# A two-block network on one core: value products of head pairs in turns, the residual written out, the RWKV mixer in 64x64 quarters

## The chip, the core and the metric

The kernel runs on one core of a Trainium2 chip. The core has five engines with a queue each: TensorE (PE, the matrix array; PEld in the profile is its weight load), VectorE (DVE), ScalarE (ACT), GpSimd (POOL) and SyncE (SP), which here issues the DMA transfers between memory (HBM) and the on-chip memory SBUF. Results of PE go to the eight banks of PSUM. The metric is the device time of one execution in microseconds, as the median of several.

## The reference, cut to what matters

A sequence of 512 tokens of width 1024 goes through two blocks of two layers. A layer of the first block joins neighbourhood attention (NA), grouped-query attention and a spatial gating; one of the second block joins four mixers, RWKV-7 among them, and a dense or an expert feed-forward part. What the change touches:

```python
def neighbourhood_attention(q, k, v, rpb):      # 8 heads of 64
    ...
    scores = scores + bias.astype(jnp.float32)
    scores = jnp.where(col_valid[:, None, :], scores, jnp.float32(-1e30))
    ...
    out = jnp.einsum('bhrqjk,brjkhd->brqhd', p, vg)
...
def gqa_attention(q, k, v):                     # 8 query heads, 2 key/value heads of 64
    ...
        sc = jnp.einsum('bqkgd,bskd->bkgqs', qi, k).astype(jnp.float32) * scale
        p = jax.nn.softmax(sc, axis=-1).astype(v.dtype)
        return jnp.einsum('bkgqs,bskd->bqkgd', p, v)
...
    return layer_norm(DEEPNORM_ALPHA * x + sub, ln_g, ln_b)   # x: the residual
...
def _rwkv7_scan(r, w, k, v, kk, a):             # 4 heads of 64, token by token
    ...
        sa = jnp.einsum('bhvk,bhk->bhv', state, -kkt)
        state = (state * wt[:, :, None, :]
                 + sa[..., None] * (kkt * at)[:, :, None, :]
                 + vt[..., None] * kt[:, :, None, :])
        return state, jnp.einsum('bhvk,bhk->bhv', state, rt)
```

## The kernel before, in words

Activations are held transposed (channels on the 128 partitions, 512 tokens along a row). All projections run as three products of split halves (`mm3`, lines 398 to 400: high by high, low by high, high by low), written `mm<-hh,wh`, `mm<-hl,wh`, `mm<-hh,wl` in the trace, with weights that SP loads in pieces of 128x1024 (`wr`) and ACT and DVE split (lines 387, 391). The core products of the mixers and attentions are fp32; such a matmul stands in the trace as two rows, a projection's as one.

Python generators issue the work: `weave` runs several side by side, each with a weight, and advances the one whose yielded costs are furthest behind its weight. A scheduler then sets the order within each engine's queue from what is ready, save where `issue_after` forces it. SP issues all loads in the order in which the program gives them; a load whose buffer is still in use holds up those behind it.

Attention. In each layer of the first block the NA stage (98 to 252 us, layer one) is woven with the projections for the other branches, the grouped-query stage (252 to 502 us) with two output branches and the spatial gating. Heads go in pairs, tokens in four blocks `a` of 128. `av_pair` scales the probabilities of both heads, transposes them (tp, line 837), copies them to `tmp` and multiplies them with the values (line 846, written `av<-tmp,gvt` or `av<-tmp,navt`): head u writes the column half u of the array, 4 key blocks in the grouped-query stage, 2 or 3 in NA. NA also needs a bias for each head, two loads `nab` that POOL negates (lines 622, 623), issued at the start of the pair that uses them. The residual H, eight tiles of 128x512, stays in SBUF over the whole layer; only the last norm of the first block writes it to memory (`spill`), after POOL has added the output bias (line 510).

RWKV. In each layer of the second block the mixer's two head pairs R(0) and R(1) are woven with the projections of two other mixers (1318 to 1500 us in layer one, 2182 to 2360 in layer two). It works on eight chunks of 64 tokens. For each head a score matrix SB over blocks of 128 tokens is made (line 1610 masks it), then the inverse of a unit triangular matrix by five doubling steps: Yp = SB T (`sc<-T,SB`), copied by DVE and ACT to Y (line 1637), Z = Y Tt (`av<-T,Y`), merged into Tt by a predicated copy of DVE (line 1642), and Tt transposed to T again (line 1647, `tp<-cst,T`). T and Tt share a tile, so the trace names both T. The tiles at, bt, rt and kt are shown as cum, a and e. Behind the loop come the products for W, G and ND, seven state steps ST (`sc<-ST,G`), further scores, and the output products `op` (`av<-SB,W`, `av<-SB,vT`, `av<-e,ST`). All these go through `mm`, line 1495.

Of the kernel before, what the change touches and what calls it, by code (L numbers as in the profile page):

```python
# [19 lines left out]
P = 128  # L20
# [19 lines left out]
RW = 58  # L40
# [9 lines left out]
SY, IY, YE, TE = 0.92, (0.5, 0.35, 0.5), (0, 1), (0, 1)  # L50
# [90 lines left out]
def host_arrays(inp):  # L141
# [25 lines left out]
    a["cst2"], a["msk2"] = _consts2()  # L167
    a["pos"] = np.ascontiguousarray(inp["positions_2"].reshape(1, S))
# [67 lines left out]
def _consts2():  # L236
# [19 lines left out]
    return np.ascontiguousarray(f), np.ascontiguousarray(np.concatenate(m, 1).astype(np.float32))  # L256

# [49 lines left out]
class K:  # L307
# [214 lines left out]

    def stats(self):
        return self.xp.tile([P, 4, 4, 6], F32, name="st", tag="st", bufs=2)


    def first_block(self):
# [9 lines left out]
        self.ln.bo = self.row(R_L + 2)  # L537
# [22 lines left out]
    def hybrid(self, l, hT):  # L560
# [51 lines left out]
        def na_attention():  # L612
            ahead = Ahead()
            nxt = both(nq[0]), *twice(nk[0])
            for i in range(4):
                av = self.bank("av")
                qs, kh, kl = nxt
                bts, mx, sm = [], [], []
                for u in range(2):
                    b0 = self.load(aps[f"nab_{l}"][2 * i + u][:, 0:384], "nab")  # L620
                    b1 = self.load(aps[f"nab_{l}"][2 * i + u][:, 384:896], "nab")
                    nc.gpsimd.tensor_scalar(b0[:, :384], b0[:, :384], -1.0, None, op0=ALU.mult)
                    nc.gpsimd.tensor_scalar(b1, b1, -1.0, None, op0=ALU.mult)
                    bts.append((b1[:, 0:256], b0[:, 0:384], b0[:, 0:384], b1[:, 256:512]))
                    x, y = stats()
                    mx.append(x)
                    sm.append(y)
                for a in range(4):
# [18 lines left out]
                    yield NY  # L647

# [163 lines left out]
        self.norm_begin(nb, nb + 1, nb + 5 + 2 if l + 1 < DEPTH else None, spill=l + 1 == DEPTH)  # L812
# [13 lines left out]
    def av_pair(self, av, a, pts, sms, nb, v):  # L826
# [5 lines left out]
        for u, (pt, sm) in enumerate(zip(pts, sms)):  # L832
# [9 lines left out]
            else:  # L842
                nc.vector.tensor_copy(t[:, :n], tp[:, :n])
        for b in range(nb):
            for u in range(2):
                nc.tensor.matmul(av[64 * u:64 * u + 64, a * P:(a + 1) * P], v(u, b), pT[u][:, b * P:(b + 1) * P],
                                 start=b == 0, stop=b == nb - 1)


    def second_block(self, hT):  # L850
# [12 lines left out]
        m64 = self.cp.tile([P, 7, 64], mybir.dt.uint8, name="m64")  # L863
        self.ident64 = self.cp.tile([P, 64], F32, name="ident64")
        for h in (slice(0, 64), slice(64, P)):
            nc.gpsimd.tensor_copy(m64[h], msk[h, :7 * P].rearrange("p (n c) -> p n c", c=P)[:, :, h])
            nc.gpsimd.tensor_copy(self.ident64[h], self.ident[h, h])
        self.lv64 = m64[:, 0]
        self.lvt64 = lambda n: m64[:, 1 + n]
# [463 lines left out]
    def mixers(self, l, hT):  # L1333
# [73 lines left out]
        def out_projection():  # L1407
            self.H = [[self.load(self.hd[j][t * P:(t + 1) * P, :], "H") for j in range(2)] for t in range(4)]
# [116 lines left out]
    def rwkv_pair(self, i, r, k, v, wa, g1, s2z):  # L1525
# [71 lines left out]

        two = [slice(0, 64), slice(64, P)]
        v64 = lambda x: x[:, :4 * 64].rearrange("p (t c) -> p t c", c=64)
        bc64 = lambda m: m.unsqueeze(1).to_broadcast([m.shape[0], 4, 64])  # L1600
        copy = (nc.scalar.copy, nc.vector.tensor_copy, nc.gpsimd.tensor_copy)
        SB, T, Tt, Y = {}, {}, {}, {}

        def score(u, w):
            x, y = ((bt, at), (bt, rt), (kt, at), (kt, rt))[w]
            ps = self.bank("sc")
            for t in range(4):
                self.mm(q(ps, t), q(x, t)[two[u]], q(y, t)[two[u]])
            z_ = self.c("SB")
            nc.vector.tensor_mul(v4(z_), v4(ps), bc4(self.masks[w % 2]))  # L1610
            return z_

        for u in range(2):
            rr = two[u]
            z_ = self.c("T")
            T[u], Tt[u] = z_[:, :256], z_[:, 256:]
            nc.gpsimd.tensor_copy(v64(T[u]), bc64(self.ident64))
            nc.gpsimd.tensor_copy(v64(Tt[u]), bc64(self.ident64))
            Y[u] = self.c("Y")
            nc.gpsimd.memset(Y[u], 0.0)  # L1620
            SB[u] = [score(u, 0)]
            yield SY
            lp = self.bank("tp")
            for t in range(4):
                nc.tensor.transpose(q(lp, t), q(SB[u][0], t), self.ident)
            for h in two:
                nc.vector.copy_predicated(v64(Tt[u])[h], bc64(self.lvt64(0)[h]), v4(SB[u][0])[h, :, h])
                nc.vector.copy_predicated(v64(T[u])[h], bc64(self.lv64[h]), v4(lp)[h, :, h])
            yield 0.5
        for n in range(1, 6):  # L1630
            for u in range(2):
# [331 lines left out]
```

## Time and profile before

| | us |
|---|---|
| median of three runs | 3246.71 (3242.65 to 3255.93) |
| profiled execution, its own time | 3253.21 |
| span of the profiled execution | 3251.4 |
| PE busy in it | 3102.4 (95%) |
| DVE busy | 1909.2 (59%) |
| ACT busy | 1338.0 (41%) |
| POOL busy | 364.0 (11%) |

The mean granted clock of PE is 0.975 of full speed. The profile lists for each engine how long it was busy; its timeline gives each instruction's start and duration, runs of equal ones on one row with their count, and in brackets how long the engine stood idle ahead of it and what released it. Durations of matmuls overlap with the next one, so the time that one takes up is read from starts.

### The profile page before, as it was taken

To read this page: it belongs to the slowest core of one execution; us is meant where nothing else is said; L and a number is where in the kernel's file an instruction comes from. 1 tells how busy PE (TensorE), PEld (TensorE's weight loads), DVE (VectorE), ACT (ScalarE), POOL (GpSimd) and SP (SyncE) were. 2 spreads that over 40 slices of the span, in tenths; PEclk is the share of its full clock that TensorE was granted. 3 is DMA by queue.
4 is the path that set the end of the run, shared out by engine and by line. 5 is a ranking of instruction groups with operands and counts; after the bars stand their busy time and mean duration, and the time that the engine had idled before them with its cause. 6 is when DMAs were issued, how large, how long until landed. Compare 5 with 4: busy or idle time off the path is not lost. (4 is left out here: it accounts for less than half of the span.)

```text
span 3251.4 us, 44427 instructions
## 1 busy us (share of the span) xinstructions
PE 3102.4 (95%) x17353; PEld 2503.6 (77%) x17353; DVE 1909.2 (59%) x3414; ACT 1338.0 (41%) x2315; POOL 364.0 (11%) x400
## 2 busy tenths in 40 slices
PE   7999999999999999999999999999999899999997
PEld 5687778877777787886657888779775588989983
DVE  6666544657745566735564333556266667777775
ACT  3534333335333333524433222343253366666652
POOL 3120000201100001003300000200042110000021
PEclk9999999999999999999999999999999899999997
DMA  4222123232221333100202333321012167877782
GB/s 160 86 84 78 59 65 115 77 114 74 83 78 58 102 105 113 57 27 27 98 20 91 92 98 99 130 80 40 27 31 90 62 225 259 257 250 257 247 285 92
DMA packets 111627, 356.87 MB, mean 110 GB/s; under 512 B 12913, under 2 KB 15985, under 8 KB 111409
## 3 DMA queue, kind: packets, MB, share of 16 engines
q1 hardware_dynamic: 108528, 344.51, 32.5%
q0 software_dynamic: 2880, 9.44, 0.8%
q8 instruction: 138, 2.26, 0.3%
q14 instruction: 81, 0.66, 0.1%
HBM read 340.40 MB, written 13.50 MB: 109 GB/s over the span
## 5 line engine op out<-in xcount | busy, mean ns | idle before, releaser
L391 DVE TENSOR_TENSOR wl<-wr,wh 128x1024 fp32r<-128x1024 f32 (+1 forms) x574 | 698.5, 1225 | 513.9 <-ACT wh L387 498.3
L387 ACT CAST wh<-wr 128x1024 fp32r<-128x1024 f32 (+1 forms) x574 | 594.2, 1045 | 754.4 <-PE mm L399 369.4
L398 PE MATMUL mm<-hh,wh 128*128 128x512 f32 (+1 forms) x1616 | 652.7, 404 | 1.3 <-DVE tmp L1462 1.2
L399 PE MATMUL mm<-hl,wh 128*128 128x512 f32 (+1 forms) x1616 | 643.9, 398 | 0.0
L400 PE MATMUL mm<-hh,wl 128*128 128x512 f32 (+1 forms) x1616 | 642.3, 398 | 0.0
L398 PEld LDWEIGHTS mm<-hh,wh 128*128 128x128 f32 (+1 forms) x1616 | 305.4, 189 | 75.8 <-issue 11.7
L400 PEld LDWEIGHTS mm<-hh,wl 128*128 128x128 f32 (+1 forms) x1616 | 305.2, 189 | 71.7 <-issue 4.2
L399 PEld LDWEIGHTS mm<-hl,wh 128*128 128x128 f32 (+1 forms) x1616 | 305.6, 189 | 70.2 <-issue 6.9
L1240 PE MATMUL mm<-xgT,wh 128*128 128x320 f32 x704 | 218.4, 310 | 0.5 <-ACT wh L387 0.3
L1240 PE MATMUL sc<-xgT,wh 128*128 128x320 f32 x704 | 218.1, 310 | 0.1
L1241 PE MATMUL mm<-xgT,wl 128*128 128x256 f32 x704 | 198.3, 282 | 4.0 <-DVE wl L391 4.0
L1241 PE MATMUL sc<-xgT,wl 128*128 128x256 f32 x704 | 196.9, 280 | 0.0
L1241 PEld LDWEIGHTS mm<-xgT,wl 128*128 128x128 f32 x704 | 132.6, 188 | 6.3 <-DVE wl L391 5.9
L431 POOL TENSOR_TENSOR rs<-rs,mhalf 128x1 f32<-128x1 f32 x36 | 32.0, 890 | 917.0 <-DVE rs L430 880.8
L1240 PEld LDWEIGHTS mm<-xgT,wh 128*128 128x128 f32 x704 | 132.7, 189 | 1.8 <-DVE xgT L1219 0.6
L1240 PEld LDWEIGHTS sc<-xgT,wh 128*128 128x128 f32 x704 | 132.5, 188 | 0.3 <-DVE tmp L1246 0.3
L1241 PEld LDWEIGHTS sc<-xgT,wl 128*128 128x128 f32 x704 | 132.7, 188 | 0.0
L398 PE MATMUL mm<-wh,hh 128*128 128x256 f32 x448 | 131.9, 294 | 0.0
L399 PE MATMUL mm<-wl,hh 128*128 128x256 f32 x448 | 130.3, 291 | 0.3 <-DVE wl L391 0.3
L400 PE MATMUL mm<-wh,hl 128*128 128x256 f32 x448 | 128.3, 286 | 0.0
L709 DVE TENSOR_REDUCE mn<-sc 128x1 f32<-128x512 f32 x64 | 44.0, 688 | 89.6 <-PE sc L706 89.6
L399 PEld LDWEIGHTS mm<-wl,hh 128*128 128x128 f32 x448 | 86.1, 192 | 5.8 <-issue 4.4
(553 smaller groups left out, 5929.1 us busy)
## 6 DMA issues: line engine op xcount, KB each, us to landing
wr<-mgu SPq DMA_DIRECT2D x176, 512.0 KB, 5.0
wr<-w SPq DMA_DIRECT2D x172, 512.0 KB, 3.7
wr<-md SPq DMA_DIRECT2D x88, 512.0 KB, 4.5
wr<-fgu SPq DMA_DIRECT2D x44, 512.0 KB, 3.7
wr<-wo SPq DMA_DIRECT2D x32, 512.0 KB, 3.8
wr<-wbr SPq DMA_DIRECT2D x24, 512.0 KB, 3.7
row<-rows SPq DMA_DIRECT2D x40, 256.0 KB, 5.4
wr<-fd SPq DMA_DIRECT2D x20, 512.0 KB, 3.7
```

The source lines that it names most:

```text
L387: nc.scalar.copy(hi[:, :n], raw[:, :n])
L391: nc.vector.tensor_sub(lo[:, :n], raw[:, :n], hi[:, :n].bitcast(F32))
L398: mm(out, lh, rh, start=first, stop=False)
L399: mm(out, lh, rl, start=False, stop=False)
L400: mm(out, ll, rh, start=False, stop=last)
L431: self.nc.gpsimd.tensor_tensor(out, out, self.mhalf, op=ALU.pow)
L709: nc.vector.tensor_reduce(mx[u][:, a:a + 1], sc, axis=AX.X, op=ALU.min)
L1240: mm(o[i][:, :2 * CAP], wh, x[:, k, :2 * CAP], start=k == 0, stop=False)
L1241: mm(o[i][:, :256], wl, x[:, k, :256], start=False, stop=k == KT - 1)
```

## The change

Value products: `av_pair` issues the heads in turns, u = 1 first, and forces all of a block's products behind its first one. NA's bias tiles are loaded and negated one head pair ahead. The residual is written to memory at the first norm and at each norm between the layers, and read back (`spilled`) ahead of branch 2. In RWKV the scores ahead of the loop are made within chunks of 64 alone, so that SB, T, Tt and Y are single tiles of 128x512 for a head pair; every product of the loop is one of 64x64 in one of the two diagonal quarters of the array (`each`); Z is computed in both orientations (`av<-Tt,Y` and `tp<-Y,Tt`) and not transposed; Y takes one copy of ACT. W, the state steps, the later scores (`full`) and the output products alternate between row or column halves; the state steps use bank tp; Q1 is padded with zeros to keep the output products in one array shape. The weave weight of R falls from 58 to 41.

```diff
-RW = 58
+RW = 41
...
-SY, IY, YE, TE = 0.92, (0.5, 0.35, 0.5), (0, 1), (0, 1)
+SY, IY = 0.9, (0.5, 0.5, 0.9)
...
-        self.ln.bo = self.row(R_L + 2)
+        self.ln.bo, self.ln.spill = self.row(R_L + 2), True
...
+            bts = bias(0)
+            nxt = both(nq[0]), *twice(nk[0])
+            for i in range(4):
...
+                if i < 3:
+                    nxt_b = bias(i + 1)
...
+        self.H = self.spilled()
         for _ in branch(2, yb, C_GQZ):
...
-        self.norm_begin(nb, nb + 1, nb + 5 + 2 if l + 1 < DEPTH else None, spill=l + 1 == DEPTH)
+        self.norm_begin(nb, nb + 1, nb + 5 + 2 if l + 1 < DEPTH else None, spill=True)
...
+        first = None
         for b in range(nb):
-            for u in range(2):
-                nc.tensor.matmul(av[64 * u:64 * u + 64, a * P:(a + 1) * P], v(u, b), pT[u][:, b * P:(b + 1) * P],
-                                 start=b == 0, stop=b == nb - 1)
+            for u in (1, 0):
+                with self.tc.issue_after(first) if first else nullcontext():
+                    i = nc.tensor.matmul(av[64 * u:64 * u + 64, a * P:(a + 1) * P], v(u, b), pT[u][:, b * P:(b + 1) * P],
+                                         start=b == 0, stop=b == nb - 1)
+                first = first or i.ins
...
-        def score(u, w):
-            x, y = ((bt, at), (bt, rt), (kt, at), (kt, rt))[w]
-            ps = self.bank("sc")
-            for t in range(4):
-                self.mm(q(ps, t), q(x, t)[two[u]], q(y, t)[two[u]])
-            z_ = self.c("SB")
-            nc.vector.tensor_mul(v4(z_), v4(ps), bc4(self.masks[w % 2]))
-            return z_
...
+        def each(out, lhsT, rhs):
+            for b in range(8):
+                for h in two:
+                    self.mm(v8(out)[h, b], v8(lhsT)[h, b], v8(rhs)[h, b])
+
+        def score(x, y, dst):
+
+            for u in range(2):
+                ps = self.bank("sc")
+                for t in range(4):
+                    for i2, h in enumerate(two):
+                        ts = slice((2 * t + i2) * 64, (2 * t + i2) * 64 + 64)
+                        self.mm(v64(ps)[h, t], x[two[u], ts], y[two[u], ts])
+                nc.vector.tensor_mul(v8(dst)[:, 4 * u:4 * u + 4], v64(ps), bc64(self.strict64))
...
         for n in range(1, 6):
-            for u in range(2):
-                Yp = self.bank("sc")
-                for t in range(4):
-                    self.mm(v64(Yp)[:, t], q(SB[u][0], t), v64(T[u])[:, t])
-                y = Y[u]
-                for i2, h in enumerate(two):
-                    copy[YE[i2]](v4(y)[h, :, h], v64(Yp)[h])
-                yield IY[0]
-                Zt = self.bank("av")
-                for t in range(4):
-                    self.mm(v64(Zt)[:, t], q(y, t), v64(Tt[u])[:, t])
-                nc.vector.copy_predicated(v64(Tt[u]), bc64(self.lvt64(n)), v64(Zt))
-                if n < 5:
-                    yield IY[1]
-                    tp = self.bank("tp")
-                    for t in range(4):
-                        nc.tensor.transpose(q(tp, t)[:64], v64(Tt[u])[:, t], self.ident)
-                    for i2, h in enumerate(two):
-                        copy[TE[i2]](v64(T[u])[h], v4(tp)[:64, :, h])
-                yield IY[2]
+            Yp = self.bank("sc")
+            each(Yp, SB, T)
+            nc.scalar.copy(Y, Yp)
+            yield IY[1]
+            Zt = self.bank("av")
+            each(Zt, Y, Tt)
+            if n < 5:
+                Z = self.bank("tp")
+                each(Z, Tt, Y)
+                nc.vector.copy_predicated(v8(T), bc8(self.lv64(n)), v8(Z))
+            nc.vector.copy_predicated(v8(Tt), bc8(self.lvt64(n)), v8(Zt))
+            yield IY[2]
...
+        def full(x, y, w):
+
+            ps = [self.bank("sc") for _ in range(2)]
+            for t in range(4):
+                for u in range(2):
+                    self.mm(q(ps[u], t), q(x, t)[two[u]], q(y, t)[two[u]])
...
         op = self.bank("av")
-        for u, rr in enumerate(two):
-            for t in range(4):
-                o = q(op, t)[rr]
-                self.mm(o, W2[:, t, rr], q(later[u, 1], t), True, False)
-                self.mm(o, tv[:, t, rr], q(later[u, 3], t), False, False)
...
+        for t in range(4):
+            o = [q(op, t)[rr] for rr in two]
...
+            for u, rr in enumerate(two):
+                self.mm(o[u], tv[:, t, rr], q(later[u, 1], t), False, False)
+            for c in (2 * t, 2 * t + 1):
+                for u in range(2):
+                    if c:
+                        self.mm(o[u][:, c % 2 * 64:c % 2 * 64 + 64], ST[:, c, :], Q1[u][:, c * 64:c * 64 + 64], False, c % 2 == 1)
```

A score of 128x512 that is masked with `strict64`, two sets of masks of 64 and a constant load for them (`cst3`) come with it. W, G, ND and Q1 keep their formulas.

What this makes of PE's queue, where the first block of value products of the grouped-query attention stands among projections (before, then after):

```order
L400 MATMUL mm<-hh,wl 128x512
L846 MATMUL av<-tmp,gvt 64x128
L398 MATMUL mm<-hh,wh 128x512
L399 MATMUL mm<-hl,wh 128x512
L400 MATMUL mm<-hh,wl 128x512
L398 MATMUL mm<-hh,wh 128x512
L846 MATMUL av<-tmp,gvt 64x128 x7
L399 MATMUL mm<-hl,wh 128x512
```

```order
L406 MATMUL mm<-hh,wh 128x512
L407 MATMUL mm<-hl,wh 128x512
L408 MATMUL mm<-hh,wl 128x512
L868 MATMUL av<-tmp,gvt 64x128 x8
L406 MATMUL mm<-hh,wh 128x512
L407 MATMUL mm<-hl,wh 128x512
```

The first product stood four projections ahead of its seven fellows; now eight stand together.

PE in the middle of the RWKV loop of the first layer (SB, T, Tt, Y as above; the rows of both head pairs follow each other), before:

```order
L1495 MATMUL av<-T,Y 128x64 x8
L1495 MATMUL sc<-T,SB 128x64
L1647 MATMUL tp<-cst,T 64x128 x8
L1495 MATMUL sc<-T,SB 128x64 x7
L398 MATMUL mm<-hh,wh 128x512
L399 MATMUL mm<-hl,wh 128x512
L400 MATMUL mm<-hh,wl 128x512
L1495 MATMUL av<-T,Y 128x64 x8
L398 MATMUL mm<-hh,wh 128x512
```

and after:

```order
L408 MATMUL mm<-wh,hl 128x256
L1521 MATMUL sc<-T,SB 64x64 x32
L1521 MATMUL av<-Tt,Y 64x64 x16
L1521 MATMUL tp<-Y,Tt 64x64 x16
L1521 MATMUL av<-Tt,Y 64x64 x16
L1521 MATMUL tp<-Y,Tt 64x64 x16
L1521 MATMUL sc<-T,SB 64x64 x32
L1521 MATMUL av<-Tt,Y 64x64 x16
L1521 MATMUL tp<-Y,Tt 64x64 x16
L1521 MATMUL av<-Tt,Y 64x64 x16
L406 MATMUL mm<-wh,hh 128x256
```

Products over 128 rows of the array with 64 columns become twice as many or more of 64x64, the transposes (`tp<-cst,T`) go, and in the middle no projections (mm) stand between the steps.

SP in the NA stage of the first layer, the third pair's bias loads before, and what stands at the same place after, where it is the fourth pair's:

```order
L386 DMA wr<-w_0 128x1024 x3
L372 DMA row<-rows 128x512 x4
L363 DMA nab<-nab 128x384
L363 DMA nab<-nab 128x512
L363 DMA nab<-nab 128x384
L363 DMA nab<-nab 128x512
L386 DMA wr<-w_0 128x1024 x3
L363 DMA nab<-nab 128x384
```

```order
L394 DMA wr<-w_0 128x1024 x2
L380 DMA row<-rows 128x512 x4
L394 DMA wr<-w_0 128x1024
L371 DMA nab<-nab 128x384
L371 DMA nab<-nab 128x512
L371 DMA nab<-nab 128x384
L371 DMA nab<-nab 128x512
L394 DMA wr<-w_0 128x1024 x6
```

The fourth pair's loads moved ahead past three weight loads.

## Rows read from the trace of the kernel before

**Rows 1.** Windows: stretch, length, busy us (x instructions) of five engines, PEclk, DMA share, GB/s

```profile
252.00:502.00 250.00, 248.29 (x1290) 197.22 (x1290) 137.36 (x219) 88.44 (x149) 5.07 (x4) 0.97 0.21 69
...
1318.00:1500.00 182.00, 179.52 (x1407) 150.16 (x1406) 89.36 (x169) 58.81 (x112) 5.39 (x12) 0.99 0.11 36
...
sum 3251.00, PE 3102.42 PEld 2503.61 DVE 1909.23 ACT 1338.01 POOL 364.00; mean PE 172.36 PEld 139.09 DVE 106.07 ACT 74.33 POOL 20.22
```

**Rows 2.** Timeline of PE in the grouped-query attention: start, us, engine, line, operation

```profile
273.82 0.40 PE L400 MATMUL mm<-hh,wl 128*128 128x512 f32 x1
274.15 0.43 PE L846 MATMUL av<-tmp,gvt 128*64 128x128 f32 x2
274.51 0.50 PE L398 MATMUL mm<-hh,wh 128*128 128x512 f32 x1
274.85 0.39 PE L399 MATMUL mm<-hl,wh 128*128 128x512 f32 x1
...
275.63 1.09 PE L846 MATMUL av<-tmp,gvt 128*64 128x128 f32 x14
276.64 0.50 PE L399 MATMUL mm<-hl,wh 128*128 128x512 f32 x1
```

**Rows 3.** Instructions of the value products' line: count, duration ns min/median/max, first to last

```profile
L846 PE MATMUL av<-tmp,gvt x512: 272/273/324, 274.2 to 1104.3; 128*64 128x128 f32 x171
...
L846 PE MATMUL av<-tmp,navt x320: 272/273/477, 120.5 to 861.4; 128*64 128x128 f32 x160
```

**Rows 4.** Waits of PE, 100 to 250 us: line and releaser, us, times, longest

```profile
PE tp L837 <- DVE prob L834: 9.0, 4, 4.7
```

**Rows 5.** Timeline of all engines, 215 to 232 us, idle and releaser in brackets

```profile
220.20 0.42 DVE L639 CUSTOM_DVE_ANT_0 prob<-sc,nab 128x256 f32<-128x256 f32 x1 [2.80 <-POOL nab L623]
...
227.70 0.41 PE L837 MATMUL tp<-cst,prob 128*128 128x128 f32 x2 [3.00 <-DVE prob L834]
```

**Rows 6.** Timeline of SP's queue, 80 to 250 us

```profile
168.01 3.24 SPq L363 DMA_DIRECT2D nab<-nab  x4
...
212.96 2.80 SPq L363 DMA_DIRECT2D nab<-nab  x4
```

**Rows 7.** Windows of PE alone: length, busy (x instructions), PEclk, DMA share, GB/s

```profile
229.00:232.00 3.00, 3.00 (x15) 0.58 0.41 145
1484.00:1497.00 13.00, 13.00 (x83) 1.00 0.00 1
```

**Rows 8.** Timeline of POOL, 8 to 60 us

```profile
30.74 10.78 POOL L510 TENSOR_TENSOR H<-H,row 128x512 f32<-128x512 f32 x5 [1.87 <-ACT H L507]
```

**Rows 9.** Timeline of PE in the RWKV mixer, 1378 to 1396 us

```profile
1388.89 1.03 PE L1647 MATMUL tp<-cst,T 128*64 128x128 f32 x8
1389.76 1.90 PE L1495 MATMUL sc<-T,SB 128*128 128x64 f32 x16
1391.46 0.48 PE L398 MATMUL mm<-hh,wh 128*128 128x512 f32 x1
```

**Rows 10.** Timeline of PE in the RWKV mixer, 1460 to 1506 us

```profile
1460.75 1.16 PE L1495 MATMUL sc<-e,e 64*128 64x128 f32 x8
1461.84 0.51 PE L400 MATMUL mm<-hh,wl 128*128 128x512 f32 x1
...
1467.07 0.45 PE L1495 MATMUL sc<-ST,G 64*64 64x64 f32 x8
...
1470.65 0.33 PE L1495 MATMUL sc<-ST,G 64*64 64x64 f32 x4
1470.91 0.43 PE L1495 MATMUL av<-SB,W 128*64 128x128 f32 x2
...
1478.29 1.16 PE L1495 MATMUL sc<-e,a 64*128 64x128 f32 x8
```

**Rows 11.** Groups by form, 1318 to 1510 us: shapes xcount, busy us, mean ns, idle before

```profile
L1642 DVE COPY_PREDICATED T<-m,av 128x256 f32<-128x256 uint8 x20 | 8.9, 444 | 11.1 <-PE av L1495 10.9
...
L1739 ACT COPY gn<-av 128x512 f32<-128x512 f32 x2 | 1.2, 585 | 12.5 <-PE av L1495 12.5
```

More of the change, by code (lines that the diff above doesn't have):

```diff
@@ L256, in _consts2, with _consts3 @@
     return np.ascontiguousarray(f), np.ascontiguousarray(np.concatenate(m, 1).astype(np.float32))
+def _consts3():
+    i = np.arange(64)
+    m = [(i[:, None] < i[None])] + [_level(s)[:64, :64] for s in LEVELS[:6]]
+    return np.ascontiguousarray(np.tile(np.concatenate(m, 1), (2, 1)).astype(np.float32))
 V_L = 0
@@ L521, in add_resid, with spilled @@
         nc.vector.bn_stats(st[:, t, j, :], h)
+    def spilled(self):
+        return [[self.load(self.hd[j][t * P:(t + 1) * P, :], "H") for j in range(2)] for t in range(4)]
     def stats(self):
@@ L613, in na_attention, with bias @@
             ahead = Ahead()
[L614 to L618, printed above, removed]
+            def bias(i):
+                out = []
                 for u in range(2):
@@ L1407, in out_projection @@
         def out_projection():
-            self.H = [[self.load(self.hd[j][t * P:(t + 1) * P, :], "H") for j in range(2)] for t in range(4)]
+            self.H = self.spilled()
             yh, yl = self.xp.tile([P, KT, S], F32R, name="yh", tag="hh"), self.xp.tile([P, KT, S], F32R, name="yl", tag="hl")
@@ L1613, in rwkv_pair @@
-        for u in range(2):
[L1614 to L1623, printed above, removed]
-            for t in range(4):
-                nc.tensor.transpose(q(lp, t), q(SB[u][0], t), self.ident)
+        bc8 = lambda m: m.unsqueeze(1).to_broadcast([P, 8, 64])
@@ L1626, in rwkv_pair @@
+        SB, T, Tt, Y = (self.c(n) for n in ("SB", "T", "Tt", "Y"))
+        nc.gpsimd.tensor_copy(v8(T), bc8(self.ident64))
+        nc.gpsimd.tensor_copy(v8(Tt), bc8(self.ident64))
+        score(bt, at, SB)
+        yield SY
+        lp = self.bank("tp")
+        for b in range(8):
             for h in two:
-                nc.vector.copy_predicated(v64(Tt[u])[h], bc64(self.lvt64(0)[h]), v4(SB[u][0])[h, :, h])
-                nc.vector.copy_predicated(v64(T[u])[h], bc64(self.lv64[h]), v4(lp)[h, :, h])
@@ L1702, in rwkv_pair @@
                     self.mm(pv[rr, 0, t], W1[h, t, rr], tb[h, t, rr])
+                for rr in two:
                     self.mm(pv[rr, 1, t], tb[h, t, rr], W2[h, t, rr], True, False)
+                for rr in two:
                     self.mm(pv[rr, 1, t], tk[h, t, rr], tv[h, t, rr], False, True)
@@ L1706, in rwkv_pair @@
             nc.vector.tensor_mul(ND[:, i2::2, :], pv[:, 1], Dc[:, i2::2].unsqueeze(2).to_broadcast([P, 4, 64]))
-            yield 1.6
+        yield 1.4
         later = {}
+        def full(x, y, w):
+            ps = [self.bank("sc") for _ in range(2)]
+            for t in range(4):
+                for u in range(2):
+                    self.mm(q(ps[u], t), q(x, t)[two[u]], q(y, t)[two[u]])
+            for u in range(2):
+                later[u, w] = self.c("SB")
+                nc.vector.tensor_mul(v4(later[u, w]), v4(ps[u]), bc4(self.masks[1]))
         ST = self.c("ST").rearrange("p (c v) -> p c v", v=64)
+        Q1 = self.cs(2, "Q1")
+        for u in range(2):
+            nc.gpsimd.memset(Q1[u][two[1 - u]], 0.0)
         nc.gpsimd.tensor_copy(ST[:, 1, :], ND[:, 0, :])
         for c in range(1, 7):
-            ps = self.bank("sc")
+            ps = self.bank("tp")
             for rr in two:
```

88 lines of the change are left out of this document (47 added, 41 removed).

## Prediction

> **What bounds the kernel now.** I read the windows by stage first. TensorE (PE) is busy 3102 of 3251 us, and in the two stages that hold most of the changed work, the grouped-query attention (252 to 502) and the RWKV mixer of the first layer (1318 to 1500), it is busy 248.3 of 250 and 179.5 of 182 us, while VectorE (DVE) works about half of the time [rows 1]. The second layer's stages repeat them. So in these stages a microsecond of PE's queue is a microsecond of the program, and the question is what each matmul occupies there, from its start to the start of the next. A PE row's own duration is no measure of that, since neighbours overlap: a plain 128x512 projection matmul is listed with 0.39 us and starts every 0.23 us in that stretch. Everything below is start to next start. [...]
>
> **Value products (av_pair).** The timeline shows one product alone at 274.15, and the other seven of its block at 275.63 [rows 2]. The lone one: the last projection before it starts at 273.82 and would be followed after 0.23 us, at 274.05; the first one after it starts at 274.51 and then holds PE until 274.85, 0.34 us where 0.23 is usual. So the lone product delays the projections by 274.85 - 0.23 - 274.05 = 0.57 us, 0.10 on the way in, 0.36 itself, 0.11 on the way out. The block of seven takes 276.64 - 275.63 = 1.01 us. Head 1 has four products there and head 0 three; the heads write different column halves of the array and run side by side, so the eighth product fills the free place beside head 1's fourth, at no cost. Each block changed to eight therefore saves 0.57 us; if the eighth were not free it would cost at most one place, 1.01/8 = 0.13. There are 512 + 320 rows of this line [rows 3], 16 per block in the grouped-query attention and on average 10 in the neighbourhood attention (NA): 32 blocks each, over both layers. Grouped-query: 32 x 0.57 = **18.2 us**, all on the path by rows 1. NA: as much at most; its stage has PE waiting for DVE [rows 4], and what is saved ahead of a wait is only waited for longer. I take 13, between 0 and 18.
>
> **NA bias a pair earlier.** At 220.20 DVE had sat idle 2.80 us for the negated bias, and some 7 us later PE stands 3.00 us for a DVE result [rows 5]. The cause is SP's queue: this pair's loads are issued at 212.96, behind weight loads that wait for buffers, and the third pair's at 168.01 [rows 6]; the changed order puts the fourth pair's loads at the third's place, 45 us earlier. After the gap the granted clock is 0.58 for at least 3 us [rows 7], the lower level, which costs another 3 x 0.42 = 1.3 us. Gain 0 to 4.3 per layer; I take **4, 8 in both**. The other waits of rows 4, the longest of 4.7 us at the start of the stage, keep their order of work, and I leave them. What is next late there is DVE.
>
> **Residual written out.** Two more sets of eight stores go into SP's queue, ahead of weight loads, and each waits for POOL's addition, the last of which ends at 30.74 + 10.78 = 41.5 us in the first norm [rows 8]. Weight loads queued behind move by some microseconds there and, likewise, at the start of the second layer. Earlier loads cover PE for a while; uncovered it costs up to 3 us each. I take **1 each, +2**. The eight reloads ahead of branch 2 go to buffers that the residual held all along before, hence free ones, with their latency under a whole branch's projections: nothing, up to +2. The freed buffers could let loads go out earlier; PE in these stages waits for none, so no gain is put down.
>
> **RWKV in quarters, per layer.** Before, by starts [rows 9, 10]. Both pairs' loop has 160 rows each of the products that make Y and Z (written sc<-T,SB and av<-T,Y): 16 of them hold PE 1391.46 - 1389.76 = 1.70 us, 0.106 each, so 320 cost 34.0. Eight blocks of eight transposes at 0.87: 7.0. Sixteen blocks of scores (four kinds, two heads, two pairs) at 1461.84 - 1460.75 = 1.09: 17.4. Eighty rows of the first transposes and the two products behind the loop, at the same 0.106: 8.5. The output products of a pair, where the array's shape changes with nearly each, 1478.29 - 1470.91 = 7.4, twice: 14.8. Sum 81.7. About 35 stretches of such work between projections pay 0.10 + 0.11 at their two ends, as the lone product did: 7.4. Together **89.1**. The state steps, their G and ND products and the product into Q1 cost about the same on both sides and are left out.
>
> After: two 64x64 products in the two diagonal quarters. The trace has just these in the state steps: four rows (two products) hold PE 0.26 us, eight add 0.45 - 0.33 = 0.12 [rows 10]. So one costs 0.06 us, and a block 0.14 on top. Per layer the changed code has 576 of them (160 + 160 + 128 in the loop, 32 each for first transposes, two scores and the product behind the second): 34.6. The product for W has 32 of 64x128, at about (1.09 - 0.14)/4 = 0.24 a piece alone and 0.12 two at once: 3.8. The later scores are 32 of 64x128 in alternating row halves and two banks: 3.8 if they overlap, 7.6 if not; I take 5.7, since no row shows it. The output products stay in one array shape and alternate columns: 32 x 0.12 + 28 x 0.06 = 5.5. Blocks: 31 x 0.14 = 4.3. About 22 stretches at 0.21: 4.6. Sum **58.5**, so 30.6 less per layer, 61 in both (57 to 65 by the later scores; the loop alone gives 34.0 + 7.0 - 448 x 0.06 = 14).
>
> Against it stands a chain. In the loop's middle the new order has no projections between the steps of the two pairs, so the evictions are uncovered. One pair's step is three blocks of 0.94 us on PE, one ACT copy of 128x512 (0.59, the nearest row being a copy of that size) and one predicated copy of 128x512 on DVE; the row has 0.444 us for half of that size, hence 0.5 to 0.89 [rows 11]. With about 0.2 for each of four hand-overs, my estimate, that is 2.8 + 0.6 + 0.9 + 0.8 = 5.1 us against 2 x 2.8 = 5.6 of PE work of both pairs: it just fits. I put 1 us there and 1.5 for the state steps at the end, where little is left to put between them: +2.5 per layer, **+5** (0 to 20). With this the mixer gives -61 + 5 = -56.
>
> **Sum.** -18 - 13 - 8 + 2 - 56 = **-93** us. The profiled run took 3253.2 us (span 3251.4), so it would take 3160; against the median of 3246.7, **3153**.
>
> **Rivals.** (1) *Quarters one after the other.* If two diagonal quarters could not run side by side, each 64x64 product would cost its 0.06 once more, 576 x 0.06 = 35 per layer, 70 in all: 3223. The state steps speak against it: their two quarters write one bank, and eight rows cost only 0.12 more than four; but no block there is longer than eight rows, and the new ones have 16 and 32. The Trainium skill, "TensorEngine Tiling (Array Packing)", section "Gotcha 1: PSUM Pressure", says that different row tiles cannot access the same PSUM bank simultaneously, which would give this result; rows 10 disagree with it as far as they go. 5 in 100. (2) *The gain is waited away.* If the predicated copy and the hand-overs sit at their upper ends, or projections on DVE get in between, each step of the loop loses 1 to 2 us and the tail 4; with NA's saving lost as well that is some 20 + 13: about 3188. For it: NA already waits for DVE, and the projections no longer stand in the loop. Against it: DVE has half its time free in the mixer and loses four small copies per pair and step. 17 in 100. (3) *Slower, by the clock.* If waits inside the quarter products bring the granted clock to its lower level there, as it was 0.58 behind the gap in rows 7, and it stayed there through all of these, the 58 us per layer double: +117 - 93 = +24, 3271. It decides when over 80% of that work runs at the lower level. Against it: 1484 to 1497, almost only narrow products, had 1.00 [rows 7]. 2 in 100. (4) *It does not do what it says*: lone products would come back. The order has none, every block stands whole; then only the attention's 31 us would go, 3184. 2 in 100. (5) *More than forecast*: later scores overlap, no waits, all of NA's share: -65 - 18 - 18 - 9, about 3137. 14 in 100.
>
> **How the numbers follow.** 60 in 100 for the forecast, within about 18 us either way (3135 to 3171), by the sizes above. To hold 8 in 10 the range takes in case 5 and case 2: 3120 to 3196. A measurement tells a change from none at about 0.5%, 16 us, so faster means under 3230: all cases but the clock and a part of the first. Faster 0.95, same 0.03, slower 0.02.
>
> **What would show it.** No lone rows of the value products, blocks of 8 to 16 rows at 1.0 us for sixteen; no 3 us gap late in the NA stage; the three kinds of quarter blocks at 0.94 to 1.1 us each for sixteen products, from start to next start; PE gaps in the mixer's loop under 0.5 us; granted clock near 1.00 there. The prediction is wrong if a block of sixteen quarter products takes 1.9 us, if PE sits idle over 10 us more in the mixer, or if the first norm's weight loads make PE wait.

## The result

The changed kernel takes 3158.1 us (median of four, 3153.5 to 3172.6) where the kernel before takes 3247.7: a ratio of 0.9726 (95% interval 0.9693 to 0.9759), 89.6 us less. Forecast were 93 less and 3153. The sum was nearly right; the terms of the bias and of the residual were not, and one was missing.

The profiled execution of the changed kernel took 3172.6 us, the slowest of the four. A second profile of the same kernel took 3159.7; where the two differ is told below. The engines, from the page of the first (share of the span, instructions):

```profile
PE 3013.7 (95%) x18729; PEld 2454.5 (77%) x18729; DVE 1889.4 (60%) x3318; ACT 1316.5 (42%) x2257; POOL 355.8 (11%) x377
```

PE still fills its queue; it has 89 us less work in it (3102 in [rows 1]) with more instructions.

**Value products.** The timeline of PE in the grouped-query attention, the first block:

```profile
266.31 0.40 PE L408 MATMUL mm<-hh,wl 128*128 128x512 f32 x1
266.64 1.09 PE L868 MATMUL av<-tmp,gvt 128*64 128x128 f32 x16
267.66 0.50 PE L406 MATMUL mm<-hh,wh 128*128 128x512 f32 x1
268.00 0.40 PE L407 MATMUL mm<-hl,wh 128*128 128x512 f32 x1
```

These are the rows that answer to [rows 2]. The lone product is gone, and sixteen rows (eight products) hold PE 1.02 us, as fourteen did: the eighth product was free.

**Quarters.** The timeline of PE in the RWKV loop of the first layer, against [rows 9]:

```profile
1355.75 1.10 PE L1521 MATMUL av<-Tt,Y 64*64 64x64 f32 x32
1356.68 1.10 PE L1521 MATMUL tp<-Y,Tt 64*64 64x64 f32 x32
1357.62 1.10 PE L1521 MATMUL av<-Tt,Y 64*64 64x64 f32 x32
...
1381.58 1.97 PE L1521 MATMUL sc<-AV,Tt 64*64 64x128 f32 x32
1383.42 1.15 PE L1521 MATMUL sc<-T,SB 64*64 64x64 f32 x32
...
1428.97 1.16 PE L1521 MATMUL sc<-e,e 64*128 64x128 f32 x8
1430.05 1.12 PE L1521 MATMUL sc<-sh,ld 128*128 128x512 f32 x2
```

(Dots mark rows left out; the last pair is from the end of the stage.) In a row of blocks one of sixteen quarter products takes 0.93 us, 0.058 a product, as forecast; one that stands alone among projections takes 1.07 (below, beside the run in another order). Sixteen products for W take 1.84, 0.115 each, also as forecast. Four later scores (eight rows) take 1.08, which is (1.08 - 0.14) / 4 = 0.235 each, as for a product alone: these row halves, four of one and then four of the other, do not overlap.

The evictions that take turns with them, by the groups of the mixer's stretch (count, busy us, mean ns, idle before), and what PE waited for there (us, times, longest):

```profile
L1669 DVE COPY_PREDICATED Tt<-m,av 128x512 f32<-128x512 uint8 x10 | 7.1, 721 | 6.6 <-PE av L1521 6.6
L1668 DVE COPY_PREDICATED T<-m,tp 128x512 f32<-128x512 uint8 x8 | 5.9, 733 | 17.8 <-PE tp L1521 17.7
L1661 ACT COPY Y<-sc 128x512 f32<-128x512 f32 x10 | 5.8, 584 | 16.0 <-PE sc L1521 16.0
```

```profile
PE sc L1521 <- DVE ND L1729: 0.4, 1, 0.4
PE av L1521 <- ACT Y L1661: 0.2, 1, 0.2
```

The predicated copy of double size takes 0.73 us, between the bounds of [rows 11], and the chain fits: PE waited 0.6 us where 2.5 were put down.

**Stage by stage.** The table gives how much longer (+) or shorter (-) each stage got, from the starts of the same PE instruction at its ends in both traces (NA: from the first transposed q, k, v to the last projection of the spatial gating's inputs; grouped-query: from there to the last value product; and so on). The singles are the first four experiments below.

| us against before | changed | changed, 2nd profile | products alone | residual alone | bias alone | quarters alone |
|---|---|---|---|---|---|---|
| up to NA, layer 1 | +3.9 | +0.1 | -0.1 | 0.0 | +1.2 | +0.1 |
| NA, layer 1 | -9.4 | -9.4 | -5.0 | -1.6 | +0.3 | +0.5 |
| grouped-query, layer 1 | -8.5 | -8.4 | -8.4 | -6.2 | -0.9 | -0.6 |
| NA, layer 2 | -8.6 | -10.2 | -2.9 | -3.3 | +0.2 | +1.0 |
| grouped-query, layer 2 | -1.1 | -8.8 | -9.5 | -0.2 | +0.6 | +7.4 |
| mixer with RWKV, layer 1 | -33.5 | -34.5 | +0.3 | -0.5 | -1.2 | -34.4 |
| linear cores, layer 1 | +9.4 | +5.8 | -0.6 | -0.4 | -0.3 | +5.7 |
| mixer with RWKV, layer 2 | -32.6 | -32.8 | 0.0 | +1.0 | +0.6 | -32.8 |
| linear cores, layer 2 | +2.9 | +2.3 | -5.8 | -4.2 | -1.1 | +3.0 |

Some of these steps are the granted clock and not the work. In the second layer's grouped-query stage the changed kernel's two profiles differ by 7.7 us; the windows of PE alone (stretch, length, busy us and instructions, granted clock, DMA share, GB/s) of the first profile, and its timeline there:

```profile
948.00:952.00 4.00, 3.97 (x22) 0.61 0.07 28
952.00:956.00 4.00, 4.00 (x20) 0.50 0.00 0
956.00:960.00 4.00, 4.00 (x19) 0.50 0.00 0
960.00:964.00 4.00, 4.00 (x21) 0.50 0.00 0
```

```profile
948.03 2.26 PE L775 MATMUL sc<-sgv,ld 128*128 128x64 f32 x13 [1.92 <-DMA ld<-sgw]
```

and of the second profile:

```profile
943.00:947.00 4.00, 4.00 (x37) 1.00 0.14 48
947.00:951.00 4.00, 4.00 (x36) 1.00 0.00 0
```

```profile
942.79 3.42 PE L775 MATMUL sc<-sgv,ld 128*128 128x64 f32 x29 [1.37 <-DMA ld<-sgw]
```

The same products of the spatial gating ran at the lower clock (0.50) in one execution, behind a wait of 1.92 us, and at the full one in the other, behind one of 1.37. I price such stretches as PE's busy time in slices of 4 us times (1 - granted clock): 8.3 us in that stage, and over the program 57 us in the profile of before, 69 and 58 in the two of the changed kernel. It is an estimate: it takes PE's work to be twice as long at 0.50 (projections start every 0.43 us where the clock is 0.50, at 38 us of the first profile, and every 0.23 at 1.00), and a slower PE also hides waits. Less that price, the changed kernel is 92 and 94 us shorter than before.

### The profile page after: what moved, and what is told of

Its sections match the earlier page's. It is cut to its first block, busy times and chain, and to the rows that moved or that the text cites. A ratio compares the mean times of both kernels' runs of the same rounds, so it can differ in the third digit from the quotient of the medians.

```text
span 3170.8 us, 46930 instructions
## 1 busy us (share of the span) xinstructions
PE 3013.7 (95%) x18729; PEld 2454.5 (77%) x18729; DVE 1889.4 (60%) x3318; ACT 1316.5 (42%) x2257; POOL 355.8 (11%) x377
## 5 line engine op out<-in xcount | busy, mean ns | idle before, releaser
L1521 PE MATMUL sc<-lE,lxk 128*128 128x128 f32 (+1 forms) x336 | 65.3, 338 | 25.4 <-ACT lE L355 11.6
```

What stands on the lines that cost most here:

```text
L1521: self.nc.tensor.matmul(out, lhsT, rhs, start=start, stop=stop)
```

## The experiments

**The four parts, each alone in the kernel before.** Their edits are the parts of the diff above: the products' order in `av_pair`; the residual (`spill` set at the first norm and between the layers, `spilled`); `bias(i + 1)`; and all of RWKV with its weights and constants.

> The kernel before with the new order of the value products alone. Theory: every lone product cost 0.57 us, so the 32 blocks of the grouped-query attention give 18 us and those of the neighbourhood attention most of theirs; about -27 us, 3221, with -9 us in each grouped-query stage. Rival: the neighbourhood attention's share is only waited for longer (its PE waits for DVE): -18 us, 3230. If the free place beside head 1's last product were not free, -14.

Measured: 3221.8 us against 3246.6 of the runs of before beside it, -24.8 (ratio 0.9932, 0.9915 to 0.9948). Both grouped-query stages give 8.4 and 9.5, 18 us as counted. NA gives 5.0 and 2.9 where 6.5 each were put down: its PE has 2.1 and 0.9 us more idle time than before. So a part of it was waited for, and the truth lies between theory and rival. In layer two low clock hides another part: by the price it is 5.7 us there, where before had 3.2.

> The kernel before with the residual written out and read back in both attention layers, and nothing else. Theory from the trace after: weight loads behind the first norm's stores come late, PE waits 2.0 us at 37 us and its clock falls for a few us behind that: +4 us, 3252, all of it ahead of 45 us, nothing in the second layer. Rival: the freed buffers let loads run ahead, so that it is the same or faster, 3240 to 3248.

Measured: 3237.3, -9.3 us (0.9973, 0.9963 to 0.9983). The rival held. Nothing is lost at the first norm, and both NA stages get shorter, by 4.9 us together. The 6.2 us of the first grouped-query stage in the table are low clock: 6.9 us by the price before, none here. SP's queue in the first NA stage, and the two largest waits of PE between 100 and 250 us:

```profile
183.33 27.26 SPq L386 DMA_DIRECT2D wr<-w  x3
210.64 1.85 SPq L363 DMA_DIRECT2D nab<-nab  x4
```

```profile
PE tp L841 <- DVE prob L838: 7.0, 3, 4.6
PE tp L841 <- DVE sm L837: 0.8, 1, 0.8
```

The last bias loads go out at 210.6, in the same order as in [rows 6] but 2.3 us earlier, and take 1.85 us to issue where they took 2.80. The waits of SP's own queue ahead of the bias loads, between 80 and 250 us, before and then here:

```profile
SPq L363 <- DVE mn L639: 1.9, 1, 1.9
SPq L363 <- PE sc L636: 1.7, 1, 1.7
SPq L363 <- PE tp L688: 0.3, 1, 0.3
```

```profile
SPq L363 <- PE mm L400: 0.3, 1, 0.3
SPq L363 <- DMA wr<-w: 0.3, 1, 0.3
```

Before, the bias loads waited 3.9 us for DVE and PE; here 0.6 in all. The residual's tiles and the bias tiles come from one pool of buffers (`c`), so it fits that eight free buffers let these loads go out earlier; no run frees buffers without writing the residual. The 3.0 us gap of [rows 5] has gone with that; the wait for prob sums to 7.0 where [rows 4] has 9.0.

> The kernel before with the bias of the neighbourhood attention loaded a head pair ahead, and nothing else. Theory: the 3.0 us gap at 227.7 and the low clock behind it go, in both layers, but two more us are lost at the stage's start, where eight tiles are loaded and negated instead of four: -4 us, 3244. Rival: the residual still holds its eight buffers, so the loads made earlier take buffers from the weights and PE waits for these: +5 to +20.

Measured: 3248.7 (1.0009, 0.9995 to 1.0023). No change, neither the theory's -4 nor the rival's +5. The three largest waits of PE in the same stretch:

```profile
PE sc L683 <- ACT tmp L347: 6.2, 1, 6.2
PE sc L641 <- DVE mn L645: 3.8, 2, 3.3
PE tp L845 <- DVE prob L842: 1.5, 1, 1.5
```

The late gap is gone and two others stand for it: 6.2 us at the start of the stage for ACT, where there were 4.7 for DVE, and 3.3 us at 205 us. It was a trade; no wait of PE for weights is among them.

> The kernel before with the quarters of the RWKV mixer alone. Theory: each mixer stage gets 33 us shorter (30.6 by the count), and the linear cores behind it give 3 to 9 us back, since ACT's queue there is in another order: -55 us, 3193, with PE waiting some 5 us more behind each mixer. Rival: the giving back came from the first block's changes and goes without them: -66 us, 3182.

Measured: 3200.3, -46.3 us (0.9856, 0.9839 to 0.9872). The mixers give 34.4 and 32.8, the linear cores take 5.7 and 3.0 back: the rival, that this came from the first block, is out. In this profile the second grouped-query stage, where the edit changes nothing, is 7.4 us longer, with 6.8 us of low clock by the price where before had none; that is most of what is missing to the theory's 55. The weave weight of R went with the quarters here and was not run apart from them.

The four singles sum to -78 us by medians, the whole is -90. By the stages NA is where they add to more than their sum (-18.0 and -19.6 in the two profiles, -10.8 as singles); why they do, no run shows.

**Quarters in another order.** In `each`:

```diff
...
-            for b in range(8):
-                for h in two:
-                    self.mm(v8(out)[h, b], v8(lhsT)[h, b], v8(rhs)[h, b])
+            first = None
+            for h in two:
+                for b in range(8):
+                    with self.tc.issue_after(first) if first else nullcontext():
+                        i = self.mm(v8(out)[h, b], v8(lhsT)[h, b], v8(rhs)[h, b])
+                first = i.ins
```

> The changed kernel with the products of the doubling loop issued in another order: the eight of the upper left quarter, then the eight of the lower right one. Theory: two quarters that follow each other in turns run side by side, though they write one bank, and in this order they cannot: a block of sixteen takes 1.9 us instead of 0.93, 28 such blocks per layer, +26 us per layer, 3210. Rival: quarters of different rows never share a bank at one time, the block was serial before and stays at 0.93: 3158.

Measured: 3198.7 (median of two), +40.6 us against the changed kernel, +18 in each mixer. A block that stands alone, in PE's timeline here and then in the changed kernel:

```profile
1341.17 1.90 PE L1521 MATMUL sc<-T,SB 64*64 64x64 f32 x32
1343.00 0.50 PE L406 MATMUL mm<-hh,wh 128*128 128x512 f32 x1
```

```profile
1334.91 1.15 PE L1521 MATMUL sc<-T,SB 64*64 64x64 f32 x32
1335.98 0.51 PE L406 MATMUL mm<-hh,wh 128*128 128x512 f32 x1
```

It takes 1.83 us where it took 1.07, with the same products into one bank. So two quarters of different rows do run side by side though both write one bank, when they alternate in the queue, and not when eight of one stand ahead of eight of the other. The rival falls, and with it the rule weighed in the forecast (the Trainium skill, "TensorEngine Tiling (Array Packing)", section "Gotcha 1: PSUM Pressure"): this measurement differs from it. It was 18 and not 26 per layer: the 26 took 0.93 for every block, and blocks in a row overlap at their seams, where the trace has rows of both blocks in turns.

**Later scores in turns.** In `full`, every product is held behind the one before it, u = 1 first:

```diff
...
+            last = None
             for t in range(4):
-                for u in range(2):
-                    self.mm(q(ps[u], t), q(x, t)[two[u]], q(y, t)[two[u]])
+                for u in (1, 0):
+                    with self.tc.issue_after(last) if last else nullcontext():
+                        i = self.mm(q(ps[u], t), q(x, t)[two[u]], q(y, t)[two[u]])
+                    last = i.ins
```

> The changed kernel with the later scores forced to alternate between the two row halves, where the order of the changed kernel has four of one half and then four of the other (16 rows in 1.7 us). Theory: row halves in two banks run side by side like the quarters; a group of 16 rows then takes 0.9 us, four groups a layer, less what the first one costs that now stands alone: -2 us per layer, 3154. Rival: halves of 64 rows and all 128 columns do not overlap; no gain, and the lone first product costs 0.3 us each, 3160.

Measured: 3143.8 (0.9687, 0.9671 to 0.9703), 14 us faster than the changed kernel, but not where theory or rival looked. The products overlap now:

```profile
1397.11 1.16 PE L1521 MATMUL sc<-e,e 64*128 64x128 f32 x14
1398.20 0.51 PE L408 MATMUL mm<-hh,wl 128*128 128x512 f32 x1
```

Seven products in 1.09 us, (1.09 - 0.14) / 7 = 0.136 each instead of 0.235. But a first product stands alone each time, and the mixer stages are as long as without the edit or longer (-33.1 and -30.1 against before). The gain lies in the linear cores (-2.4 and -5.1 against before, where the changed kernel has +9.4 and +2.9) and in the first grouped-query stage, where no low clock came.

**The order on ACT in the linear cores.** In the changed kernel the first linear cores begin with this wait; ACT's row of its releaser stands below it:

```profile
1463.86 3.75 PE L1521 MATMUL sc<-lE,lxk 128*128 128x128 f32 x16 [5.05 <-ACT lE L355]
...
1462.81 3.41 ACT L355 ACTIVATE lE<-le,cst 128x256 f32<-128x256 f32 x8
```

Eight scaled copies (lE) stand in one row, behind the exponentials of three steps, where before they went out in twos. The edit holds each step's exponentials behind the last step's scaled copies:

```diff
...
-            self.act(lv(e)[:, :, s:], lv(Pf)[:, :, s:], AF.Exp)
-            self.act(lv(e)[:, :, :s], lv(X)[:, :, :s], AF.Exp)
+            with self.tc.issue_after(last) if last else nullcontext():
+                self.act(lv(e)[:, :, s:], lv(Pf)[:, :, s:], AF.Exp)
+                self.act(lv(e)[:, :, :s], lv(X)[:, :, :s], AF.Exp)
...
-                            self.act(ev[:, :, h], half(e), AF.Identity, scale=self.heads[nh][:, h:h + 1])
+                            last = self.act(ev[:, :, h], half(e), AF.Identity, scale=self.heads[nh][:, h:h + 1]).ins
```

> The changed kernel with one order forced on ACT in the linear cores: a core's exponentials of the next step not ahead of its scaled copies of this one. Theory: the wait of 5.05 us at the start of the linear cores is ACT's order (eight scaled copies stood behind the exponentials of three steps), so it and the low clock behind it go: -5 to -10 us, 3150, nearly all behind the first mixer. Rival: the chain of POOL, ACT and DVE is late in any order, since the mixer now ends earlier and less projection work is left to cover it: within 2 us of 3158.

Measured: 3166.1 (0.9742, 0.9717 to 0.9768), not told apart from the changed kernel (0.9726, 0.9693 to 0.9759). The wait fell from 5.05 to 1.02 us, and in the profile the stage got longer all the same. PE's idle time in it hardly moved, 20.6 us where the changed kernel has 21.9 and 20.1: as the rival says, the chain is late in this order too, in more and shorter waits. The whole stage in windows (length, busy of five engines, PEclk, DMA share, GB/s) of before, of the changed kernel, of this one and of the one with the later scores in turns:

```profile
1498.00:1712.00 214.00, 196.91 (x935) 135.37 (x934) 134.77 (x274) 90.72 (x192) 62.21 (x79) 0.99 0.15 50
```

```profile
1440.00:1664.00 224.00, 202.11 (x940) 140.97 (x939) 138.31 (x275) 91.72 (x192) 62.65 (x80) 0.96 0.15 48
```

```profile
1422.00:1656.00 234.00, 213.36 (x927) 147.63 (x928) 134.39 (x273) 89.84 (x191) 61.47 (x80) 0.91 0.14 46
```

```profile
1422.00:1632.00 210.00, 190.67 (x919) 132.69 (x918) 133.15 (x273) 89.61 (x190) 61.73 (x79) 1.00 0.15 51
```

The granted clock is what differs most: 0.91 here, 1.00 in the last. By the price above low clock cost 1.7 us of this stage before, 6.9 in the changed kernel (4.5 in its second profile), 21.9 with the forced order and nothing with the later scores in turns. My theory, that the long wait brings the low clock, falls: this kernel has no wait over 1.9 us in the stage and the most low clock, in the one profile taken of it.

**The bias at its old place.** The changed kernel without `bias(i + 1)`:

> The changed kernel with the bias of the neighbourhood attention loaded at the start of its own head pair again. Theory: the earlier loads only traded the late gap for a longer first one (6.2 us where it was 4.7) and another at 206 us; without them the stage is as short or 2 us shorter in each layer: 3152 to 3158. Rival: with the residual's buffers free the earlier loads do pay, and the stages lose 4 us each: 3166.

Measured: 3158.1 (0.9727, 0.9710 to 0.9743), the same as with it. PE's gaps over 0.8 us between 95 and 250 us sum to 8.9 us against 11.1, the stage is 1.9 us longer all the same (137.1 for 135.2). It is worth nothing here either way.

**Repeats and a sum.** Two more profiles, of the changed kernel and of the one with later scores in turns, and that one with the bias at its old place:

> The changed kernel itself, profiled a second time. Theory: the waits of PE are the same to 0.2 us (6.2 us at the start of the neighbourhood attention, 5.05 us in the first linear cores), and so is the low clock right behind the longest of them, while the low clock of 15 to 20 us at the spatial gating of the grouped-query stage (it was there in both layers) and that at 1544 us come and go by chance: stages differ by 5 to 9 us there and by under 1 us elsewhere. Rival: all low stretches are in the same places, so they are part of the change's price.

> The changed kernel with the later scores forced to alternate between row halves, profiled a second time. Theory: its 14 us against the changed kernel came from the linear cores, half of it by shorter waits (2.7 us where there were 5.05), which return, half by low clock that happened to be missing, so that this run lies at 3140 to 3150 with some low clock in the linear cores. Rival: the order in its linear cores avoids the low clock each time: none there again, 3135.

> The changed kernel with the later scores forced to alternate and the bias of the neighbourhood attention loaded at the start of its own pair. Theory: the two edits touch different stages and the bias one is worth nothing: 3142 to 3146. Rival: the shorter first wait of the neighbourhood attention (4.6 us for 6.2) counts once the rest is at rest: 3138.

Measured: 3159.7, 3136.2 and 3161.7. The waits repeat: 6.24 us at the start of NA (6.22 in the first profile), 4.17 for 5.05 in the linear cores. The low clock does not come purely by chance: in the first grouped-query stage the changed kernel had it in both its profiles (6.5 us each), the kernel with the scores in turns in neither, nor in its first linear cores. So the rival of the second expectation (3135, none there again) holds for that build. But the third kernel has the same waits in its first linear cores (2.68 and 1.71 us) and 11.7 us of low clock there, so the order of those scores is not its reason. Against the runs of before beside it that kernel stands at 0.9726 (0.9701 to 0.9751), the one with the bias early at 0.9687: some 13 us were lost by an edit of another stage that is worth nothing by itself.

**A wait ahead of the spatial gating.** Two lines moved, the loads of the gating's weights, from the start of `spatial_gating` to ahead of the grouped-query stage:

```diff
+        wsT = [self.load(aps[f"sgw_{l}"][:, j * S:(j + 1) * S]) for j in range(2)]
         weave((gqa_attention(), WB[0]), (chain(branch(0, ya, C_NAZ), spatial_gating(), branch(1, yc, C_SGZ)), WB[1]))
...
         def spatial_gating():
-            wsT = [self.load(aps[f"sgw_{l}"][:, j * S:(j + 1) * S]) for j in range(2)]
```

> The changed kernel with the two loads of the spatial gating's weights moved ahead of the grouped-query stage. In the changed kernel its first product waits 1.4 to 2.1 us for them in both layers, and PE ran 15 to 20 us at the lower clock right behind that wait in three of four cases. Theory: that low clock is set off by the wait; without the wait it is gone in both layers: -3.5 us for the waits and -6 to -12 for the clock, 3146. Rival: these products, narrow and fp32, run at the lower clock by chance with no wait ahead of them: -3.5 us, 3155.

Measured: 3143.5 (0.9669, 0.9646 to 0.9692), 14.6 us faster than the changed kernel. Its windows over the same products:

```profile
349.00:353.00 4.00, 4.00 (x34) 1.00 0.25 95
353.00:357.00 4.00, 3.41 (x22) 1.00 0.01 4
```

The grouped-query stages are 17.3 and 10.5 us shorter than before, with the clock at 1.00 in both, and 1.4 us of idle time in the two together (4.7 in the changed kernel). This agrees with the theory, in one profile; the time agrees in four executions. It doesn't show that the wait brings the clock down: with the scores in turns the same products waited 1.4 and 1.8 us (1.4 and 1.9 in its second profile) and kept it, and with the order on ACT 1.4 and 1.4. Over the fourteen profiles, two layers each, these products stand 21 times behind a wait of 1.3 to 2.1 us; the clock fell to 0.50 there 11 times and stayed at 1.00 10 times. In the seven cases with a wait of 0.9 us or less or none it stayed at 1.00.

## Why the prediction was right

- **What bounds it, and start-to-start prices**: right. Where a stage is full of PE work, the count came out: 18 us of 18.2 in the grouped-query stages, 33 a mixer where 30.6 less 2.5 of waits were put down. Blocks of quarter products cost 0.93 in a row and 1.07 alone, where the forecast's own 0.06 and 0.14 make 0.96 and 1.10 (its 0.94 does not follow from them); W's cost 0.115 of 0.12. The later scores cost the upper bound (0.235 each) and not the middle. What came out better can be read in the first mixer stage of both traces: PE's idle time fell from 7.3 to 6.5 us where 2.5 more were put down, and between projections there are 26 stretches of products of `mm` and of the mixer's transposes where there were 49 (22 and 35 in the forecast). From start to start these products take 81.1 us where they took 110.6, and the projections, with 659 rows for 662, 138.8 for 141.1.
- **Value products in NA**: the mechanism was right, the size not: 8 us alone where 13 were put down. The term's own bound, that what is saved ahead of a wait is waited for, took more, and low clock some of it in layer two. With the other parts NA gave 18 to 20 in all, close to the 13 + 8 that the two terms said together, but not for the reason of the second.
- **Bias a pair earlier**: wrong, 0 for -8. The step that failed is "the other waits keep their order of work, and I leave them". With the bias early the scheduler put DVE's work in another order, and new waits took what the late gap gave. DVE and PE in the kernel with the bias early alone, and the same splits before:

```profile
201.59 2.34 DVE L609 TENSOR_TENSOR kl<-naqkv,kh 64x512 fp32r<-64x512 f32 x2
203.96 0.69 DVE L750 BATCH_NORM_STATS2 ss<-sgv 128x6 f32<-128x512 f32 x1
204.57 0.41 DVE L645 CUSTOM_DVE_ANT_0 prob<-sc,nab 128x256 f32<-128x256 f32 x1
...
205.04 0.44 PE L641 MATMUL sc<-kh,qs 128*128 128x384 f32 x1 [3.34 <-DVE mn L645]
```

```profile
187.31 1.39 DVE L609 TENSOR_TENSOR kl<-naqkv,kh 64x512 fp32r<-64x512 f32 x2
```

  Two splits (kl) that ran at 187 us now stand ahead of the score reduction (prob, with its mn) that PE waits for. The first wait, 6.2 us where it was 4.7, cost little by contrast: the transposes that ended it before now run ahead of it, and the product behind it starts 20.8 us into the stage where it started 20.4.
- **Residual written out**: wrong in sign, -9 for +2. The failed step is "PE in these stages waits for none, so no gain is put down". PE's own row named DVE, and DVE's named POOL [rows 5]; behind these stood SP, whose bias loads went out late [rows 6], 3.9 us of it waiting for DVE and PE. Of the 9 us the NA stages show 5; the first grouped-query stage's part is clock, seen in one profile. The stores, put at 1 each, cost nothing when alone, but not always: in the first profile of the changed kernel the weights behind them come late, a sign of being wrong that the forecast named, and in the second half as late.

```profile
37.32 0.67 PE L408 MATMUL mm<-hh,wl 128*128 128x512 f32 x1 [1.98 <-DVE wl L399]
```

```profile
36.71 0.50 PE L408 MATMUL mm<-hh,wl 128*128 128x512 f32 x1 [0.93 <-DVE wl L399]
```

  The stage up to NA is 3.9 and 0.1 us longer there. PE waits 0.9 us or more at this place in four of the ten profiles with the stores and in none without.
- **RWKV**: the mechanism was right, -46 alone of -56. The mixers gave 67 in that profile, more than forecast. A term was missing: the linear cores behind them, where nothing was changed, took 8 to 12 us back, and in some runs low clock elsewhere took more. In the changed kernel's first linear cores PE's idle time is 3.0 to 4.8 us above before, the low clock by the price 2.8 to 5.2; in the second layer it is idle time alone (3.1 to 3.7). That the order there would be another was to be seen in the new order of ACT's queue; what clock it would get was not.
- **The rivals**: serial quarters are excluded by the order experiment; the low clock came, not in the quarter products (no row of them ran at 0.50 in either profile; the 3.0 to 4.3 us that the price gives for a mixer stage lie elsewhere in it) but in the stages around.
- That the total was right to 4 us is partly luck. Term by term the singles are 6 (value products), 10 (bias) and 10 (RWKV, with the linear cores) short of the forecast and 11 (residual) over it, 78 in all; the parts together gave 12 more than that, which no term foresaw.

## What to carry to other kernels

In a stage that one engine fills, count what each instruction occupies from start to start, the way in and out of another array shape included: that count held to 10%. Where an engine waits, follow the wait back to its first cause before pricing a fix, and expect the next wait to take most of it; a buffer set free did more here than a load moved. And an edit that reorders one stage reorders its neighbours too, so compare whole programs, twice, with the clock beside them.

## What the hardware showed that was not expected

- Products in two diagonal quarters overlap within one PSUM bank if they alternate in the queue (1.07 us for sixteen in a block alone), and not if eight of one stand ahead of eight of the other (1.83). Row halves with all 128 columns, in two banks, do the same: 0.136 us a product in turns, 0.235 in groups of four.
- The granted clock cost 43 to 73 us of a program by the price used here. At the same products it was 1.00 or 0.50 for up to 17 us, by execution or by build, with waits of 1.3 to 2.1 us ahead in both cases. With that wait taken away there was no low clock in either layer, but two builds that kept the wait had none either; in the linear cores a shorter wait went with more of it. What decides it there stays open.
